# Query, key and gate products token-major as seven products of eight, retention chunk by chunk inside the last weight set, HGRN alone in stage two

## The chip, the cores and the metric

The kernel runs on one core of a Trainium2 chip. Its engines are TensorE (PE in the profile, with its weight loads as PEld), VectorE (DVE), ScalarE (ACT), GpSimd (POOL) and SyncE (SP), which here only starts transfers. Each engine runs its own queue of instructions in order. The metric is the device time of one execution in microseconds (us); of several executions the median is given. All times in this document are microseconds unless marked ns.

## What is computed

One layer of a hybrid decoder, for a prompt of 2048 tokens and for 8 single decode tokens, with a model width of 1024, all in float32:

```python
p = rmsnorm(x, norm_g) @ w_in                    # (2048, 1024) @ (1024, 4096)
rq, rk, rv, rg, hq, hf, hi, hgate = split(p, 8)  # 512 columns each: 4 heads x 128
# retention: rotary positions on q and k, a fixed decay per head
rq, rk = rotary(rq), rotary(rk) * 128 ** -0.5
o_ret = recurrence(rq, rk, rv, log_gamma)        # S = gamma*S + k v^T,  o = S^T q
o_ret = head_rmsnorm(o_ret, ret_g) * silu(rg)
# HGRN2: decay per channel, from the forget gate
f = lb + (1 - lb) * sigmoid(hf)
k = (1 - lb) * sigmoid(-hf)
o_hg = recurrence(silu(hq), k, hi, log(f))       # S = diag(f)*S + k v^T
o_hg = head_rmsnorm(o_hg, hg_g) * silu(hgate)
y = rmsnorm(x + concat(o_ret, o_hg) @ w_out, final_norm_g)
```

The states after the last token are outputs too. The decode tokens start from given states and go through the same formulas, one step each.

## The kernel before

**Products.** Every float32 operand of a large product is split into a rounded high part, written by ScalarE (`hi_lo`, L106), and the rest, written by VectorE (L107). A product of two such operands is three TensorE matmuls, high by high, high by low and low by high (`three`, L303, L305). Below, "plain" is a product done that way. "Seven products" is one step of a Strassen scheme: a product of 2x2 blocks is made from seven block products of sums of blocks instead of eight. The list is

```python
PRODUCTS = [("A11", "B11"), ("A12", "B21"), ("S2", "T2"), ("S3", "T3"), ("S1", "T1"), ("S4", "B22"), ("A22", "T4")]
```

where A is a pair of 128-token chunks (S1 to S4 its sums, made by `tok_ops` and split by `s_split`) and B the weights (T1 to T4 their sums, made by `wv_comb`). One block product is 4 x 3 = 12 matmuls of 128x512.

**The order of work.** TensorE's queue is in the order of the program's text; the queues of the other engines are ordered by a scheduler that works from the program's data. Work wrapped in `behind` (L115) is placed after the latest instruction of VectorE, ScalarE and SyncE at that point of the text.

**Stage one** computes the two value groups, rv and hi, token-major (tokens on the partitions): eight pairs of 256 tokens, in the order `V_ORDER`. Two pairs are plain, with 96 matmuls each, and six go through `v_pair` (L307) with 84. The seven results pass through seven rotating PSUM banks, VectorE adds them up, and the values are stored in `v_dram`. Norm factors (`stats`, `spread`) and splits for the next pairs are placed between the products.

**Stage two** has 16 units: for each half of the prompt (1024 tokens) and each of four head numbers, one HGRN head and then one retention head.

```python
for half in range(2):
    for h in range(NH):
        order += [(half, 1, h), (half, 0, h)]
```

A unit first computes three groups of its head feature-major (features on the partitions), plain, in segments of 512, 256 and 264 tokens in the first half, where the 264 hold the eight decode tokens, and 512 and 512 in the second (`seg_steps`, L578). The tiles are `pjqr`, `pjkr` and `pjg` for retention, `pjfh`, `pjqh` and `pjg` for HGRN. VectorE and ScalarE evacuate them: rotary tables for retention (`ret_proj`, L630), sigmoids for HGRN and gates (L612, L652 to L665). Then comes its scan. For retention: scores per chunk (L757). For HGRN: seven levels of updates, each multiplying key and query by products of forget gates (L811), kept copies by ScalarE (L821, L822), and small score products put through masks (L841, L847). Both end in `tail_steps`: key transposes (L683), key-value products (L690), the chain of states on VectorE (L698), outputs (L705, L707), squares on ScalarE (L711), the norm factor on GpSimd (L102, L103), one scaling of 128x512 (L715), output transposes (L721), a product with the gate (L723) and a store to `o_dram` (L726).

The scan of unit i is woven into the matmuls of unit i+1. `merge` walks the matmuls and puts in a scan step when its share of the work is due:

```python
while n < len(rec) and (need + rec[n][0]) * span * total <= at * due:
    need += rec[n][0]
    rec[n][1]()
    n += 1
```

Side work has places in units (`side_at`): sums of the output weights (`t_sum`, `t_spool`) and the eight decode states, with a load (`d_load`), two VectorE products, a sum and a TensorE product (`d_mm`, tile `pd`, L403). Splits of the next tokens (`x_steps`) and of the output weights (`wo_steps`) are woven into certain units.

**Stage three** is the output projection over `o_dram` and the weights: two plain chunks and seven pairs as seven products (tile `po`), the residual, the last norm, and a product for the decode tokens (`pyd`, L403), in which four strips of the 128 rows hold four column blocks.

Of the kernel before, what the change touches and what calls it, by code (L numbers as in the profile page):

```python
# [10 lines left out]
F32 = mybir.dt.float32  # L11
# [30 lines left out]
def step_kernel(ctx, tc, a, out):  # L42
# [8 lines left out]
    ps_pj = ctx.enter_context(tc.tile_pool(name="ps_pj", bufs=3, space=PSUM))  # L51
    ps_lv = ctx.enter_context(tc.tile_pool(name="ps_lv", bufs=2, space=PSUM))
    ps_o = ctx.enter_context(tc.tile_pool(name="ps_o", bufs=2, space=PSUM))
    ps_tr = ctx.enter_context(tc.tile_pool(name="ps_tr", bufs=1, space=PSUM))
# [5 lines left out]
    v_dram = [  # L60
        [dr.tile([CH, P, GW], F32, tag=f"v_dram{n}{ty}", name=f"v_dram{n}{ty}") for ty in range(2)]
        for n in range(2)
# [34 lines left out]
    rst = const.tile([P, T - 512], F32, name="rst")  # L97
    const.tile([P, 56], F32, name="fill")
    dq, dk, df, dg_ = (const.tile([P, 8, NB], F32, name=f"d{n}") for n in "qkfg")
# [28 lines left out]
    order = []  # L128
    for half in range(2):
        for h in range(NH):  # L130
            order += [(half, 1, h), (half, 0, h)]
    want = []
    for half, ty, h in order:
        for g in ((RQ, RK, RG), (HF, HQ, HG))[ty]:
            want.append(g * NH + h)
# [18 lines left out]
    x_cur = {}  # L154

    def x_alloc(blk):
        n = 528 if blk == 1 else 512
        x_cur[blk] = tuple(
            xp.tile([P, KT, n], F32R, tag=f"x{t}{blk % 2}", name=f"x{t}{blk}") for t in "hl"
        )  # L160

    def x_load(blk, kp):
        r = rawp.tile([P, 2, 512], F32, tag="raw", name=f"xr{blk}{kp}")
        for j in range(2):
            sp.dma_start(
                r[:, :, j * 256 : j * 256 + 256], a["x_t"][2 * blk + j, :, 2 * kp : 2 * kp + 2]
            )
        return r

    def x_split(blk, kp, r):  # L170
        xh, xl = x_cur[blk]
        rb = rst[:, (blk - 1) * 512 : blk * 512]
        for j in range(2):
            k = 2 * kp + j
            dve.scalar_tensor_tensor(
                r[:, j], r[:, j], g_in[:, k : k + 1], rb, op0=ALU.mult, op1=ALU.mult
            )
# [5 lines left out]
    V_ORDER = [4, 5, 6, 7, 2, 3, 0, 1]  # L183
    vctx = ExitStack()
    vq = vctx.enter_context(tc.tile_pool(name="vq", bufs=1))
    x_alloc(0)
    xh0, xl0 = x_cur[0]
# [18 lines left out]
    def bank(shape, name):  # L206
        pl, tag = ((ps_pj, "pj"), (ps_lv, "lv"), (ps_o, "o"))[(0, 1, 2, 0, 1, 2, 0)[bank_n[0] % 7]]
        bank_n[0] += 1
        return pl.tile(shape, F32, tag=tag, name=name)
# [3 lines left out]
    def tok_load(i):  # L213
        p = V_ORDER[i]
        xr[i] = [rawp.tile([P, 4, 2 * P], F32, tag="raw", name=f"xr{p}{j}") for j in range(2)]
        for j, r in enumerate(xr[i]):
            sp.dma_start(r, a["x_t"][p, :, 4 * j : 4 * j + 4])
# [1299 lines left out]
```

## Time and profile before

| | |
|---|---|
| median of 3 runs | 1065.55 (1065.42 to 1066.16) |
| span of the profiled execution | 1062.5 |
| TensorE busy in it | 1050.9 (99%), 9107 matmuls |
| VectorE busy | 733.6 (69%) |
| ScalarE busy | 395.3 (37%) |
| GpSimd busy | 115.8 (11%) |
| moved by DMA | 149.64 MB, of that 110.14 MB in SyncE's queue |
| busy at 0 to 174.3, stage one (TensorE / VectorE) | 172.7 / 139.8 |
| 174.3 to 881.0, stage two | 705.9 / 462.2 |
| 881.0 to 1062.5, last scan and stage three | 172.3 / 131.6 |

The span runs from the first to the last instruction that the profile shows. The median of the runs is 3.05 above it. The page gives the busy time of each engine, the same in 40 slices of the span (a digit is tenths), and a chain of work that ended last, followed back from the last instruction to whatever released it. A matmul's row names the tile that it fills, the tiles that it reads and its shape. Rows of groups end in the number of instructions, their busy time, the mean ns of one, and the idle time of the engine ahead of them with what ended it. Matmul records overlap, since they are pipelined, so the distance between two starts tells what one costs.

### The profile page before, as it was taken

The numbers are of one execution on the slowest core, as the hardware profiler recorded it, in microseconds if no ns is written. First come the engines' busy times: TensorE is split into PE (matmuls) and PEld (weight loads), VectorE is DVE, ScalarE is ACT, GpSimd is POOL, SyncE is SP. The second block draws the span as 40 slices with busy tenths as digits, with TensorE's granted clock in tenths as the row PEclk, the third lists the DMA queues.
The fourth block names the chain that finished last, engine by engine and source line by source line (L and its number), as shares of the span: only waits on it lengthen the run. The fifth ranks groups of instructions, "written<-read, shape, count | busy, mean of one in ns | idle before, by whom it ended". The sixth has DMA issues, their size and how long they took to land.

```text
span 1062.5 us, 21859 instructions
## 1 busy us (share of the span) xinstructions
PE 1050.9 (99%) x9107; PEld 899.6 (85%) x9107; DVE 733.6 (69%) x1271; ACT 395.3 (37%) x859; POOL 115.8 (11%) x218
## 2 busy tenths in 40 slices
PE   9999999999999999999999999999999999999997
PEld 7788888989989999998988888888788888788775
DVE  6886986594585567457977565746855687678785
ACT  7853323242432243333443323332423244333241
POOL 1110000001000010110110101011010103311122
PEclk9999999999999999999999999999999999999999
DMA  8664346422502240361654235126323337855642
GB/s 303 208 216 156 127 139 225 166 78 100 187 34 80 87 153 2 119 202 39 200 157 122 63 108 151 40 67 182 120 67 109 108 106 268 276 187 200 220 160 99
DMA packets 103890, 149.64 MB, mean 141 GB/s; under 512 B 5872, under 2 KB 69552, under 8 KB 103024
## 3 DMA queue, kind: packets, MB, share of 16 engines
q1 hardware_dynamic: 83888, 110.14, 32.9%
q0 software_dynamic: 6960, 25.24, 6.5%
q10 hardware_dynamic: 12944, 12.88, 3.5%
q8 instruction: 71, 1.16, 0.4%
q14 instruction: 27, 0.22, 0.1%
HBM read 109.86 MB, written 38.37 MB: 140 GB/s over the span
## 4 chain that ended last, share of the span: by engine, by line
PE 91%; DMA 3%; DVE 2%; ACT 2%; issue 1%; POOL 1%; SPq 0%; DVEq 0%; POOLq 0%; ACTq 0%
PE pjg L578 17%; PE po L305 13%; PE pv L305 11%; PE pjkr L578 9%; PE pjqr L578 8%; PE pjqh L578 8%; PE pjfh L578 8%; PE plh L841 2%; DMA xn<-in_x_prompt 2%; PE py L1231 1%; PE pur L690 1%; PE par L757 1%; PE por L705 1%; PE por L707 1%; PE poh L705 1%; PE puh L690 1%
## 5 line engine op out<-in xcount | busy, mean ns | idle before, releaser
L578 PE MATMUL pjg<-xh,w_h 128*128 128x512 f32 (+2 forms) x320 | 113.9, 356 | 0.0
L578 PE MATMUL pjg<-xh,w_l 128*128 128x512 f32 (+2 forms) x320 | 111.3, 348 | 0.0
L578 PE MATMUL pjg<-xl,w_h 128*128 128x512 f32 (+2 forms) x320 | 111.0, 347 | 0.0
L106 ACT ACTIVATE w_h<-wr 128x1024 fp32r<-128x1024 f32 x48 | 50.8, 1059 | 87.5 <-PE pjg L578 33.6
L107 DVE TENSOR_TENSOR w_l<-wr,w_h 128x1024 fp32r<-128x1024 f32 x48 | 58.6, 1222 | 23.3 <-ACT w_h L106 11.4
L578 PEld LDWEIGHTS pjg<-xh,w_l 128*128 128x128 f32 x320 | 60.2, 188 | 7.9
L578 PEld LDWEIGHTS pjg<-xh,w_h 128*128 128x128 f32 x320 | 60.3, 188 | 7.1 <-issue 0.4
L578 PEld LDWEIGHTS pjg<-xl,w_h 128*128 128x128 f32 x320 | 60.3, 188 | 6.7
L578 PE MATMUL pjqr<-xh,w_h 128*128 128x512 f32 (+2 forms) x160 | 58.2, 364 | 0.0
L578 PE MATMUL pjkr<-xh,w_h 128*128 128x512 f32 (+2 forms) x160 | 57.9, 362 | 0.0
L578 PE MATMUL pjfh<-xh,w_h 128*128 128x512 f32 (+2 forms) x160 | 57.4, 359 | 0.0
L821 ACT ACTIVATE kepth<-kh 128x1024 f32<-128x1024 f32 x24 | 25.5, 1062 | 85.6 <-DVE kh L811 85.6
L578 PE MATMUL pjqh<-xh,w_h 128*128 128x512 f32 (+2 forms) x160 | 56.6, 354 | 0.0
L578 PE MATMUL pjfh<-xh,w_l 128*128 128x512 f32 (+2 forms) x160 | 55.7, 348 | 0.0
L578 PE MATMUL pjkr<-xl,w_h 128*128 128x512 f32 (+2 forms) x160 | 55.5, 347 | 0.2 <-issue 0.2
L578 PE MATMUL pjkr<-xh,w_l 128*128 128x512 f32 (+2 forms) x160 | 55.6, 347 | 0.0
L578 PE MATMUL pjqh<-xh,w_l 128*128 128x512 f32 (+2 forms) x160 | 55.6, 347 | 0.0
L578 PE MATMUL pjqr<-xh,w_l 128*128 128x512 f32 (+2 forms) x160 | 55.6, 347 | 0.0
L578 PE MATMUL pjqr<-xl,w_h 128*128 128x512 f32 (+2 forms) x160 | 55.5, 347 | 0.0
L578 PE MATMUL pjqh<-xl,w_h 128*128 128x512 f32 (+2 forms) x160 | 55.5, 347 | 0.0
L578 PE MATMUL pjfh<-xl,w_h 128*128 128x512 f32 (+2 forms) x160 | 55.5, 347 | 0.0
L612 ACT ACTIVATE sg<-pjg 128x512 f32<-128x512 f32 (+2 forms) x40 | 20.4, 510 | 75.9 <-PE pjg L578 65.9
(851 smaller groups left out, 2819.5 us busy)
## 6 DMA issues: line engine op xcount, KB each, us to landing
wr<-in_w_in SPq DMA_DIRECT2D x48, 512.0 KB, 4.8
xn<-in_x_prompt SPq DMA_DIRECT2D x32, 256.0 KB, 3.0
v_dram<-vo SPq DMA_DIRECT2D x32, 256.0 KB, 2.8
v<-v_dram SPq DMA_DIRECT2D x16, 512.0 KB, 4.8
or<-o_dram SPq DMA_DIRECT2D x16, 512.0 KB, 5.8
xro<-in_x_prompt SPq DMA_DIRECT2D x14, 512.0 KB, 3.3
out_y_prompt<-xro POOLq DMA_DIRECT2D x13, 512.0 KB, 3.0
xr<-in_x_t SPq DMA_DIRECT2D x12, 512.0 KB, 4.4
```

The lines of the kernel that those rows point to most:

```text
L106: act.activation(h, src, AF.Copy)
L107: dve.tensor_tensor(l, src, h.bitcast(F32), op=ALU.subtract)
L305: pe.matmul(ps, xx, ww, start=(first and n == 0), stop=(last and n == 2))
L578: pe.matmul(ps, ww[:, kk], x[:, k, b0 : b0 + n], start=(k == 0 and i == 0), stop=(k == KT - 1 and i == 2),)
L612: act.activation(sg[:, :n], ps, AF.Sigmoid)
L690: pe.matmul(pu[:, j], ksb[g][:, j], vcol(4 * g + j), start=True, stop=True)
L705: pe.matmul(po[:, j], A[:, c], vcol(c), start=True, stop=src is None)
L707: pe.matmul(po[:, j], qcol(c), src, start=False, stop=True)
L757: pe.matmul(pa[:, j], k[:, cc], q[:, cc], start=True, stop=True)
L821: act.activation(ss[:, 512:], k[:, :HALF], AF.Copy)
L841: pe.matmul(dst[32 * i : 32 * i + 32, c], kk, qq, start=True, stop=True)
L1231: pe.matmul(ps, o[:, kk], w[:, k % 4, i * 512 : (i + 1) * 512], start=(k == 0 and n == 0), stop=(k == KT - 1 and n == 2),)
```

## The change

Stage one gets three weight sets. Set zero is the value groups as before. Set one is rq and rg, set two rk and hgate. Each set runs over all eight token pairs, so there are 24 pairs, of which the first two are plain and 22 are seven products. Stage two is left with the two HGRN groups hf and hq of each head.

- **Products.** They accumulate in three PSUM banks, a, b and c, where a product continues its bank's sum. ScalarE copies three stages out (`s1`, `u2`, `p5`). The results that go to memory are made by `emit`: gates get their SiLU there (ScalarE sigmoid, VectorE product), queries and keys their rotation (`turn`, four VectorE operations).
- **Operands of later sets.** The scaled tokens and their sums are stored by set zero and loaded again by the later sets (`a_dram`, `s_dram`); so are the weight sums of sets one and two (`wg_load`, `wg_spool` in pairs three to six of the set before; `wg_fetch` in pair seven). Their splits (`wg_split`) stand across the boundary of two sets. Set two walks the pairs in order 0 to 7, and set one in the order 1, 2, 4, 5, 3, 6, 7, 0.
- **Decode tokens.** Their query, key and gates come from 16 products in four strips (`wg_decode`) beside the weight loads.
- **Retention.** In set two, each chunk's four heads are worked through when the pair that follows computes: load of query, value and gate; transposes of key and query (`r_flip`); scores and masks; key-value products; outputs, squares, norm factor on GpSimd and scaling with the gate; transposes back, scaling by ScalarE, store. The state of four heads stays in one tile. The last chunk's steps are merged with the first steps of HGRN unit 0.
- **HGRN.** Eight units, (half, head), in stage two; the scan's steps and weights are as before. The output's scaling takes the token-major gate in four operations of 128x128 in place of one of 128x512, and the norm weight moves to ScalarE's copy of the transposed output. `side_at` halves its positions; token splits are woven into units 0, 3 and 4, output-weight splits into unit 7. The sums T2 and T1 of the output weights load into other buffers, T1 after the last scan. The products' PSUM pool has two buffers (`ps_pj`, three before), as has that of the transposes.

The diff, cut to its core:

```diff
+    CHAIN = [("A11", "B11", "a"), ("A12", "B21", "b"), ("S2", "T2", "a"), ("S1", "T1", "c"),
+             ("S3", "T3", "a"), ("S4", "B22", "c"), ("A22", "T4", "a")]
...
+    def turn(dst, src, cs, name):
...
+        dve.tensor_tensor(
+            t1[:np_].rearrange("p (h d) -> p h d", d=64), src.rearrange("p (h d) -> p h d", d=64), c, op=ALU.mult
+        )
+        dve.tensor_tensor(u[:np_, :, 1], x[:, :, 0], sn, op=ALU.mult)
+        dve.scalar_tensor_tensor(u[:np_, :, 0], x[:, :, 1], -1.0, sn, op0=ALU.mult, op1=ALU.mult)
+        dve.tensor_tensor(dst, t1[:np_], t2[:np_], op=ALU.add)
...
+        for n, (x, w, b) in enumerate(CHAIN):
...
             if n == 0:
+                keep("s1", ps)
             elif n == 1:
+                emit(ca, 0, ps, "s1")
             elif n == 2:
+                keep("u2", ps)
             elif n == 3:
+                keep("p5", ps)
             elif n == 4:
+                emit(ca + 1, 1, ps, "p5")
             elif n == 5:
+                emit(ca, 1, ps, "u2")
             else:
+                emit(ca + 1, 0, ps, None)
...
+        if p:
+            st[0] += [lambda: r_flip(cb)]
+            st[0.5] = [lambda: r_update(cb)]
+            st[1] += [lambda: r_score(cb)]
+            st[2] += [lambda: r_out(cb)]
+            st[4] += [lambda: r_turn(cb)]
+        if more:
+            st[0] += [lambda: r_load(ca, "q")]
+            st[2] += [lambda: r_load(ca, "v"), lambda: r_flip(ca)]
+            st[3] += [lambda: r_load(ca, "g"), lambda: r_score(ca), lambda: r_update(ca)]
+            st[4] += [lambda: r_load(ca + 1, "q"), lambda: r_out(ca)]
+            st[5] += [lambda: r_load(ca + 1, "v")]
+            st[6] += [lambda: r_turn(ca), lambda: r_load(ca + 1, "g")]
...
-            dve.tensor_tensor(ob[g], po, rs.unsqueeze(2).to_broadcast([P, 4, P]), op=ALU.mult)
+            for j in range(4):
+                dve.scalar_tensor_tensor(
+                    ob[g][:, j], po[:, j], rs[:, j : j + 1], gcol(4 * g + j), op0=ALU.mult, op1=ALU.mult
+                )
...
-            dve.tensor_tensor(
-                ot, pt.rearrange("p a b -> p (a b)"), gt[:, g * 512 : (g + 1) * 512], op=ALU.mult
-            )
+            act.activation(ot, pt.rearrange("p a b -> p (a b)"), AF.Copy, scale=ng[:, hd : hd + 1])
...
-    for hd, at in enumerate((8.45, 10.02, 10.48, 12.02, 12.33, 12.63, 14.02, 14.45)):
+    for hd, at in enumerate((4.22, 5.01, 5.24, 6.01, 6.16, 6.31, 7.01, 7.22)):
...
-    for k, at in enumerate((0.5, 2.1, 4.1, 6.1)):
+    for k, at in enumerate((0.5, 1.1, 2.1, 3.1)):
```

In `r_steps`, p is the pair's number in set two, ca the even chunk of this pair and cb the odd chunk of the pair before; `st[n]` holds what follows product n of the pair, and `st[0.5]` what stands in the middle of product one.

749 lines of the change are left out of this document (454 added, 295 removed).

## The prediction

> **What bounds the kernel now.** I read the page first (busy shares, slices, chain), then the chain in order of time, then the groups by shape, then stretches.
>
> ```profile
> PE 1050.9 (99%) x9107; PEld 899.6 (85%) x9107; DVE 733.6 (69%) x1271; ACT 395.3 (37%) x859; POOL 115.8 (11%) x218
> PE   9999999999999999999999999999999999999997
> DVE  6886986594585567457977565746855687678785
> PE 91%; DMA 3%; DVE 2%; ACT 2%; issue 1%; POOL 1%; SPq 0%; DVEq 0%; POOLq 0%; ACTq 0%
> ```
>
> TensorE is busy in every slice and is 91% of the chain; VectorE has a third of the span free. So a matmul taken away is worth its full distance to the next one, as long as VectorE and ScalarE still hand over in time. Distances come from the chain in order of time (start, length, what, count) and, for small ones, from the difference of two starts in the timeline:
>
> ```profile
> 61.85 19.09 PE pv L305 x84
> 174.26 5.44 PE pjfh L578 x24
> 190.58 2.84 PE pjfh L578 x24
> 199.10 2.92 PE pjfh L578 x24
> 297.61 1.40 PE pjqr L578 x6
> 344.37 2.77 PE pjfh L578 x12
> ...
> 682.19 0.60 PE L683 MATMUL pkh<-ident,kh 128*128 128x128 f32 x4
> 682.55 0.48 PE L578 MATMUL pjkr<-xh,w_h 128*128 128x512 f32 x1
> 685.40 1.05 PE L690 MATMUL puh<-v,ksh 128*128 128x128 f32 x8
> 686.29 0.60 PE L683 MATMUL pkh<-ident,kh 128*128 128x128 f32 x4
> 996.45 1.05 PE L403 MATMUL pyd<-wd,dq 128*8 128x256 f32 x16
> 997.42 0.50 PE L305 MATMUL po<-woh,op5A11h 128*128 128x512 f32 x1
> ```
>
> A 512-column matmul costs 19.09/84 = 0.227 us, one of 256 columns 2.84/24 = 0.118, of 264 columns 2.92/24 = 0.122. Four transposes take 682.55 - 682.19 = 0.36, four fp32 128x128 products (eight records) 0.89, two decode products of four strips 0.97, so 0.485 each.
>
> **What the change takes from TensorE.** Counted in the two programs' instruction orders: 512-column matmuls go from 3108 to 3300 (+192 x 0.227 = +43.6), those of 256 and 264 columns from 576 each to 192 each (-384 x 0.118 = -45.4, -384 x 0.122 = -46.7). Together -48.5: seven products of eight, for four of the six groups that were plain. It adds 64 transposes (the query's flip; the key's flip replaces the key's old transpose): 64 x 0.09 = +5.8. The decode columns of those groups become 16 four-strip products: 16 x 0.485 = +7.8. The fp32 retention and HGRN products keep their number. Net -34.9. If nothing else moved, the span would be 1062.5 - 34.9 = 1027.6. The median of the runs, 1065.55, is 3.05 above the profiled span, and I carry that offset: 1030.7 is the floor.
>
> **What becomes late.** Most of the change is on VectorE and ScalarE, which run their queues in the order written. The durations (mean ns of one, ahead of the last bar):
>
> ```profile
> L107 DVE TENSOR_TENSOR w_l<-wr,w_h 128x1024 fp32r<-128x1024 f32 x48 | 58.6, 1222 | 23.3 <-ACT w_h L106 11.4 <-DMA t_draml<-wos11l 4.5 <-DMA t_draml<-wos21l 4.3
> L811 DVE TENSOR_TENSOR kh<-kh,fph 128x512 f32<-128x512 f32 x48 | 33.3, 694 | 2.4 <-PE plh L841 1.7 <-PE plh L891 0.3
> L698 DVE SCALAR_TENSOR_TENSOR sth<-sth,fph,puh 128x128 f32<-128x128 f32 x48 | 16.7, 347 | 9.7 <-PE puh L690 8.3
> L715 DVE TENSOR_TENSOR obh<-poh,orsh 128x512 f32<-128x512 f32 x16 | 11.1, 691 | 27.7 <-ACT jkh L711 16.9 <-POOL orsh L103 10.8
> L665 DVE TENSOR_TENSOR qth<-qh,fh 128x256 f32<-128x256 f32 x8 | 3.4, 424 | 0.2
> L654 DVE TENSOR_SCALAR fh<-fsh,lb,lb 128x512 f32<-128x512 f32 x12 | 6.5, 546 | 19.2 <-ACT fsh L652 19.2
> L657 DVE TENSOR_SCALAR kh<-fxh,lb 128x512 f32<-128x512 f32 x12 | 5.8, 486 | 0.0
> L847 DVE COPY_PREDICATED Abh<-lmask,plh 128x128 f32<-128x128 uint8 x32 | 10.7, 334 | 0.3
> L821 ACT ACTIVATE kepth<-kh 128x1024 f32<-128x1024 f32 x24 | 25.5, 1062 | 85.6 <-DVE kh L811 85.6
> L822 ACT ACTIVATE kepth<-qth 128x512 f32<-128x512 f32 x24 | 15.0, 626 | 0.0
> L612 ACT ACTIVATE sg<-pjg 128x512 f32<-128x512 f32 x24 | 14.3, 594 | 55.4 <-PE pjg L578 45.4 <-DVE dS L981 5.1 <-PE pd L403 4.8
> L711 ACT ACTIVATE jkh<-poh 128x128 f32<-128x128 f32 x64 | 17.8, 278 | 10.8 <-PE poh L707 9.3
> L711 ACT ACTIVATION_READ_ACCUMULATOR jkh<-poh 128x1 f32 x64 | 12.5, 196 | 0.0
> L103 POOL TENSOR_TENSOR orsh<-orsh,mhalf 128x4 f32<-128x4 f32 x16 | 17.6, 1097 | 1.2
> L102 POOL TENSOR_SCALAR orsh<-omsh 128x4 f32<-128x4 f32 x16 | 4.1, 257 | 281.7 <-ACT jkh L711 281.6
> ```
>
> *Retention inside the third set.* A pair of chunks gives TensorE 19.09 + 24 transposes (2.2) + 32 fp32 products (7.1) = 28.4. VectorE has about 20.6 of work, so its throughput suffices, but the work is one chain through the queues from one pair's key rotation to the next. Step by step: flips 0.72, six matmuls 1.36, a wait of 0.6 (ScalarE's two copies and four key scalings take 2.3 after the first flip), key-value products 0.89, six matmuls 1.36: 4.9. Then VectorE adds 0.69, rotates (0.69 + 0.42 + 0.42 + 0.69) and masks the score with four small operations (1.4): 4.3, and only then can the output products start: 1.79, four squares with their accumulator reads 1.9, GpSimd 1.35, four scalings 1.4: 6.4. Splits (0.69 + 1.22 + 1.22) stand in the queue ahead of the second chunk's four mask operations (1.4): 4.5. Its output again: 6.4. Split 1.22, add 0.69, sigmoid 0.59, product 0.69, rotation 2.2: 5.4. Sum 31.9, against 28.4: 3.5 late per pair, for seven pairs 25, and 3 for the first, where weight splits of 1.22 stand ahead of the key. **+28** (bounds: 0 if the queue overlaps these steps, 37 if nothing does).
>
> *HGRN alone.* The scan on TensorE is what a unit of three groups took beyond them: 344.37 - 297.61 - 3 x (5.44 + 2.84 + 2.92) = 13.2. A unit of two groups is then 22.4 + 13.2 = 35.6 in half 0, 4 x 5.44 + 13.2 = 35.0 in half 1. Before, a scan had a retention unit and its own successor beside it; now each 35 us hold one. VectorE per unit: 14 updates x 0.69 = 9.7, products of forget gates 2.2 (0.69, 0.42 and smaller), masks 2.2, eight states and eight outputs x 0.347 = 5.6, gates and queries 2 x (0.546 + 0.486 + 0.69 + 0.69) = 4.8, two weight splits 2.4: 26.9. The outputs are the one row that the change makes worse there: four of 0.347 replace one of 0.691, +0.7 each. [...]
>
> Side work now falls into half as many units: output-weight sums (4 x 0.69 + 2 x 1.22 = 5.2) in units 0 to 3, token splits (4.9) in 3 and 4, decode states (2 or 3 x 1.22 each) in 4 to 7, output-weight and first output splits (7.3) in 7. VectorE then needs 32, 32, 37, 34, 32, 37, 41 in units 1 to 7 and some 36 beside the last scan. Its queue also waits inside each unit: for the first scores 1.4, for ScalarE's two keeps after each pair of updates (1.06 + 0.63, three times, partly covered), for the two output norms. Walking unit 2 and unit 6 through the written order gives waits of about 5, and unit 4 gives 11, because its decode product stands behind an update, three splits and the decode state's own steps on VectorE. Units 1 to 7 then last 37, 37, 41, 45, 37, 41, 46 and the last scan 40 (its floor 35): late by 1.5, 1.5, 5.5, 10, 2, 6, 11 and 5. **+42** (bounds: 13, the surplus of VectorE's work alone, to 55).
>
> *First two sets and joints.* The product chain now accumulates in one bank, so the seventh product waits for VectorE's read of the fifth; with spooled weight sums ahead of it (two of 0.69 and a split) that is 1.1 late in four pairs: 4.4. Two pairs of set one redo the token sums: 3. Splits between sets one and two: 2. The first HGRN unit's second token block reuses the retention's memory, so its four splits (4.9) start after the last retention output: 4. The output weights' sum T1 loads only when the last scan releases its buffers: 2. **+15** (0 to 25).
>
> Sum: 1030.7 + 28 + 42 + 15 = 1115.7; forecast 1115.
>
> **The rivals.**
> *Waits stay hidden (faster).* TensorE remains the bound, as it is in the row of 99%; only VectorE's surplus of 13 in stage two and some 3 at the joints show: 1030.7 + 16 = 1047. It decides where all new waits together stay under 33. For it speaks that VectorE kept up in this stretch at 82%, with TensorE never idle:
>
> ```profile
> 58.00:174.00 116.00, 115.81 (x523) 95.58 (x522) 95.52 (x156) 44.93 (x73) 5.01 (x12) 1.00 0.50 166
> 565.00:655.00 90.00, 90.00 (x885) 75.52 (x888) 54.15 (x95) 28.89 (x69) 9.31 (x14) 1.00 0.33 100
> ```
>
> (columns: stretch, length, busy us of PE, PEld, DVE, ACT, POOL, granted clock, DMA share, GB/s.) Against it: there the splits served a pair ahead, while stage two's 54 of 90 become 32 to 41 of 35. Chance 0.14.
> *Half the waits:* the walks count each wait in full and some overlap: 1030.7 + 85/2 = 1073, still slower. Chance 0.2.
> *Transfers bind in the first set.* Pairs three to six move tokens, norm rows, values, spooled tokens, spooled sums, new weights and their sums: seven MiB, 7.34 MB, in 20 us, 367 GB/s. The first row above gives 166/0.50 = 332 GB/s when all engines work, so 22.1 us a pair, +8, and as much where the next set's seven MiB are fetched in one pair: 1115 + 16 = 1131. Chance 0.12.
> *Waits cost clock too.* The granted clock is 1.00 in both rows, with no idle TensorE to test it. [...] Chance 0.06.
>
> **How the numbers follow.** The forecast case has 0.48. The range of 8 in 10 leaves out most of the fastest case below and the upper bounds together above (1030.7 + 37 + 55 + 25 = 1148): 1053 to 1148. A measurement of this kernel tells about 0.2% from no change (1063.4 to 1067.7). Faster 0.14 from the first rival; same 0.04 from the low edge of half the waits; slower 0.82.
>
> **What would show it.** Right: TensorE's share falls from 99% to near 92%, with idle time ahead of the retention's output and flip products released by VectorE, and ahead of the HGRN kept-score, decode and output transposes; pairs of the third set last about 32, HGRN units 37 to 46; VectorE above 85% in stage two. Wrong: pairs of 28.5 and units of 36, or long DMA waits in the first set. The forecast falls if the whole new idle time of TensorE is under 50 us.

## The result, and the profile after

The changed kernel takes 1136.03 us (median of 4 runs, 1131.52 to 1138.34) against 1065.51 before, a ratio of 1.0653 with a 95% interval of 1.0628 to 1.0678. The profiled execution took 1131.52, 1.8 above its span of 1129.7. The forecast was 1115 with a range of 1053 to 1148: the direction and the range held, and the time is 21 above the forecast.

The page of the changed kernel: busy shares, then four of the rows of 40 slices, the transfers, and the chain that ended last, as shares of the span.

```profile
PE 1059.6 (94%) x8731; PEld 866.8 (77%) x8731; DVE 795.5 (70%) x1453; ACT 525.9 (47%) x1153; POOL 149.7 (13%) x260
PE   9999999899998999999996799997998998899997
DVE  6867756887768665566555587786668688567776
PEclk9999999999999999999998899998999998999999
DMA  8698889477778555555444934476445573865652
DMA packets 141625, 235.73 MB, mean 209 GB/s; under 512 B 10224, under 2 KB 78080, under 8 KB 141264
PE 27%; issue 6%; DVE 4%; ACT 3%; DMA 3%; POOL 2%; POOLq 0%; ACTq 0%; DVEq 0%; SPq 0%
```

TensorE is no longer full in every slice: the deepest holes are the 22nd and 23rd (unit 0, at 594 to 640), the 28th, and smaller ones between the 31st and the 35th. The granted clock falls in four of these slices; in the two stretches that the prediction showed of before it was 1.00. VectorE's share is what it was (69%, now 70%). The bytes moved grew from 149.64 to 235.73 MB, and in the first third of the span the transfers are mostly at seven to nine tenths. (The chain can be followed back only to 612 us, so its shares are of half a span.) TensorE stands idle for 1129.7 - 1059.6 = 70.1 us, where it was 1062.5 - 1050.9 = 11.6 before. Line numbers from here on are lines of the changed kernel or of the edit in question.

The stretches of the changed kernel, in the order sets zero and one, set two, unit 0, units 1 to 7, last scan, projection (columns as in the prediction: stretch, length, busy us of PE, PEld, DVE, ACT, POOL, granted clock, DMA share, GB/s):

```profile
0.00:350.70 350.70, 342.16 (x1631) 269.71 (x1632) 253.21 (x421) 164.25 (x296) 29.87 (x52) 1.00 0.79 281
350.70:594.10 243.40, 233.22 (x1324) 198.33 (x1323) 151.75 (x326) 123.68 (x347) 30.12 (x45) 0.99 0.54 174
594.10:640.10 46.00, 34.44 (x319) 30.62 (x317) 27.80 (x57) 18.53 (x42) 5.62 (x8) 0.85 0.63 204
640.10:931.60 291.50, 267.49 (x4218) 222.82 (x4209) 219.71 (x445) 147.40 (x320) 40.40 (x63) 0.96 0.54 171
931.60:980.80 49.20, 40.72 (x600) 33.12 (x598) 33.86 (x62) 24.93 (x54) 15.23 (x26) 0.92 0.54 165
980.80:1129.70 148.90, 141.58 (x655) 112.23 (x654) 109.17 (x144) 47.15 (x95) 28.44 (x67) 0.98 0.53 184
```

The boundaries are the starts of the first matmul of pair 16, of unit 0 and of unit 1, the end of unit 7's last matmul into `pjqh`, and the last HGRN output transpose. Unit lengths below are distances between such starts: 41.7, 37.5, 40.3, 52.0, 38.3, 44.6 and 37.2 for units 1 to 7.

What TensorE waited for in the changed kernel (engine, line, releaser: us in total, times, longest):

```profile
PE pkt L662 <- DVE rk L338: 11.1, 9, 5.4
PE poth L942 <- DVE obh L935: 9.7, 8, 4.9
PE pjfh L831 <- ACT fxh L873: 5.7, 1, 5.7
PE pah L1050 <- DVE qh L884: 5.5, 3, 2.3
PE pd L530 <- DVE dqp L1173: 4.8, 1, 4.8
```

These are hand-overs that the prediction named (key transposes, output transposes, first scores, decode products), and between them one product that waits for its bank's sigmoids (third row; more on it below). Behind the four longest of these, of 4.8 and more, the granted clock is 0.50 (after that of 5.7 until 627.93). The timeline of TensorE in unit 0, after its longest wait:

```profile
622.00 0.58 PE L831 MATMUL pjfh<-xh,w_h 128*128 128x256 f32 x1 [5.66 <-ACT fxh L873]
622.38 0.42 PE L831 MATMUL pjfh<-xl,w_h 128*128 128x256 f32 x1
...
627.93 0.29 PE L831 MATMUL pjqh<-xh,w_h 128*128 128x256 f32 x1
628.05 0.28 PE L831 MATMUL pjqh<-xl,w_h 128*128 128x256 f32 x1
```

Matmuls of 256 columns are 0.21 apart until 627.9 and 0.12 after it. This happens at ten places. The granted clock of those stretches is 0.50. TensorE is busy for 40.6 us in them, and half of that, 20 us, is what half speed costs it.

### The profile page after: what moved, and what is told of

Read it like the earlier page. It is cut to its first block, busy times and chain, and to the rows that moved or that the text cites. A ratio compares the mean times of both kernels' runs of the same rounds, so it can differ in the third digit from the quotient of the medians.

```text
span 1129.7 us, 22331 instructions
## 1 busy us (share of the span) xinstructions
PE 1059.6 (94%) x8731; PEld 866.8 (77%) x8731; DVE 795.5 (70%) x1453; ACT 525.9 (47%) x1153; POOL 149.7 (13%) x260
## 2 busy tenths in 40 slices
DMA packets 141625, 235.73 MB, mean 209 GB/s; under 512 B 10224, under 2 KB 78080, under 8 KB 141264
## 5 line engine op out<-in xcount | busy, mean ns | idle before, releaser
L1001 DVE TENSOR_TENSOR kh<-kh,fph 128x512 f32<-128x512 f32 x48 | 33.3, 693 | 13.2 <-PE plh L1031 12.4
L699 DVE SCALAR_TENSOR_TENSOR obr<-por,omr,rg 128x128 f32<-128x128 f32 x64 | 18.0, 344 | 34.6 <-POOL omr L697 34.6
L113 DVE TENSOR_TENSOR ab_l<-xr,ab_h 128x512 fp32r<-128x512 f32 (+1 forms) x40 | 38.1, 955 | 5.1 <-ACT ab_h L112 3.9
L831 PEld LDWEIGHTS pjfh<-xh,w_h 128*128 128x128 f32 x160 | 31.8, 199 | 11.3 <-ACT fxh L873 5.8
L112 ACT ACTIVATE ab_h<-xr 128x512 fp32r<-128x512 f32 (+1 forms) x40 | 32.5, 848 | 15.9 <-DVE xr L270 15.8
L831 PEld LDWEIGHTS pjqh<-xh,w_h 128*128 128x128 f32 x160 | 31.0, 194 | 8.6 <-ACT w_h L112 2.9
L831 PEld LDWEIGHTS pjfh<-xh,w_l 128*128 128x128 f32 x160 | 31.8, 199 | 4.5
L831 PEld LDWEIGHTS pjfh<-xl,w_h 128*128 128x128 f32 x160 | 32.0, 200 | 3.4
L113 DVE TENSOR_TENSOR w_l<-wr,w_h 128x1024 fp32r<-128x1024 f32 x16 | 19.5, 1221 | 20.9 <-ACT w_h L112 14.8
L831 PEld LDWEIGHTS pjqh<-xl,w_h 128*128 128x128 f32 x160 | 31.1, 194 | 3.0
L1523 DVE SCALAR_TENSOR_TENSOR xro<-xro,yms,fg 128x1024 f32<-128x1024 f32 (+1 forms) x15 | 18.1, 1214 | 21.2 <-POOL yms L109 21.2
L1004 DVE TENSOR_TENSOR qth<-qth,fph 128x512 f32<-128x512 f32 x48 | 32.8, 684 | 0.0
```

Of the source, the lines that this page charges most:

```text
L112: act.activation(h, src, AF.Copy)
L113: dve.tensor_tensor(l, src, h.bitcast(F32), op=ALU.subtract)
L699: dve.scalar_tensor_tensor(o[:, cc], po[:, h], ms[:, h : h + 1], rb_of[c, "g"][:, cc], op0=ALU.mult, op1=ALU.mult)
L831: pe.matmul(ps, ww[:, kk], x[:, k, b0 : b0 + n], start=(k == 0 and i == 0), stop=(k == KT - 1 and i == 2),)
L1001: dve.tensor_tensor(kv[:, :, 0, :], kv[:, :, 0, :], two[:, :, 1:2].to_broadcast([P, nb, b]), op=ALU.mult)
L1004: dve.tensor_tensor(qv[:, :, 1, :], qv[:, :, 1, :], two[:, :, 0:1].to_broadcast([P, nb, b]), op=ALU.mult)
```

## The experiments

All twelve are edits of the changed kernel, to be compared with its 1136.0; three (own buffers, scores, all together) stand each on the edit before it and are compared with that run. The times are medians, with the fastest and slowest run behind them. Lengths of stretches and units come from one profiled execution each. That of the changed kernel is the fastest of its four, and sets zero and one, which nearly all the edits leave alone, took 350.7 to 353.9 us in the profiles (but for one run, named below), so a difference of 3 us in one stretch tells nothing. The kernel before, run again beside the edits, took 1065.6 to 1067.2 us.

### Half speed: idle matmuls ahead of seven waits

```diff
+    def keep_warm(n):
+        t = ps_tr.tile([P, P], F32, tag="tr", name=f"kw{warmed[0]}")
+        for _ in range(n):
+            pe.matmul(t, ident, ident, start=True, stop=True)
...
+            if p == 0:
+                st[2] += [lambda: keep_warm(20)]
```

> The changed kernel with idle matmuls added: small fp32 products of the identity into a spare transpose buffer, placed just ahead of seven of its longest TensorE waits (20 before the first key transposes of the retention, 8 before those of its last chunk, 24 after its last output transposes, 12 before the first kept scores of unit 1, 20 before the decode product of unit 4, 8 and 20 before the second output transposes in unit 3 and in the last scan). Nothing is computed differently and no wait is removed. Theory: a wait costs twice, once for itself and once because the granted clock is 0.50 in the stretch of 3.4 us or more behind it. In the profile after, such stretches behind these seven places cost TensorE 2.0 + 1.7 + 3.0 + 1.6 + 2.7 + 1.7 + 1.4 = 14 us; they go: 1136 - 14 = 1122. Rival: what follows a wait is late through VectorE anyway, so a faster TensorE only waits longer: 1136, within 3 us.

Measured: 1135.5 (1133.0 to 1136.0). The granted clock of the changed kernel, and of this run:

```profile
core 0: 1129.7 us, clock 0.976
```

```profile
core 0: 1133.7 us, clock 0.991
```

The clock came back and the time did not. The rival holds for the sum: TensorE now waits 9.9 us at one place, the kept scores of unit 4, where the changed kernel waits 0.3 (and 4.8 and 2.5 at other places of that unit), and unit 4 is 55.7 instead of 52.0. A faster TensorE only arrives earlier at something else that is late.

### Three hand-overs moved

```diff
-            st[2] += [lambda: r_load(ca, "v"), lambda: r_flip(ca)]
+        if more and p == 0:
+            st[3] += [lambda: r_load(ca, "g"), lambda: r_flip(ca)]
...
-                if n in (1, 2, 3, 5, 7):
+                for _ in range({3: 1, 4: 2, 5: 1, 7: 1}.get(n, 0)):
...
-    wd_at[2] += [(0, d_ms), (2, d_rs), (4, d_tr)]
+    wd_at[2] += [(0, lambda: behind(d_ms)), (2, d_rs), (4, d_tr)]
```

> The changed kernel with three hand-overs moved, no work removed. One: in the first pair of set two the transposes of the first chunk, its scores and its outputs each stand one product later, its transposes back half a pair later. Two: the last chunk's steps, merged with the first matmuls of unit 0, start two matmul steps later and then follow each other closely. Three: in the last scan the decode norm's square on ScalarE stands behind what was issued before it, and GpSimd starts the loads of T1 only after the last scan's stores. Theory: each is a single late hand-over that the order of the queues makes, with the halved clock behind it: 5.4 + 2.0 at the first place, 2.5 + 1.7 and some 4 at the second, some 5 + 1.4 at the third: 22 in all: 1136 - 22 = 1114. Rival: VectorE is behind there as a whole, and the waits come back at the next hand-over: 7 less or nothing: 1129 to 1136.

Measured: 1136.2 (1133.9 to 1138.0). The first pair of set two got shorter (30.7 to 28.0) and so did unit 0 (46.0 to 44.7) and the last scan (49.2 to 47.1), but sets zero and one took 3.0 more in the profiled execution and the projection 4.6 more. The three places are 6 shorter together and the two other stretches 7.6 longer, of which the 3.0 lie where nothing was edited, so by the median the rival's "nothing" holds, and the profile can't say more.

### VectorE: less work

One edit gives an operation to ScalarE, the other halves the updates of the scans.

```diff
-            dve.tensor_scalar(k[:, tt], xr[:, :n], lb1[:, h : h + 1], None, op0=ALU.mult)
+            act.activation(k[:, tt], xr[:, :n], AF.Copy, scale=lb1[:, h : h + 1])
```

> The changed kernel with one VectorE operation of each HGRN evacuation given to ScalarE: the key's scaling by one minus the lower bound, 20 operations of 0.35 to 0.49 us, 8.6 us of VectorE in all. Theory (order of hand-overs, VectorE busy at 74% of stage two): what stands behind these operations comes earlier only where VectorE is the last: some 3 us less, 1133. Rival (VectorE's throughput bounds the units): the whole 8.6 us, 1127.

Measured: 1139.3 (1133.9 to 1141.5), no gain.

```diff
+            nh = nb // 2
-                kv[:, :, 0, :], kv[:, :, 0, :], two[:, :, 1:2].to_broadcast([P, nb, b]), op=ALU.mult
+                kv[:, :nh, 0, :], kv[:, :nh, 0, :], two[:, :nh, 1:2].to_broadcast([P, nh, b]), op=ALU.mult
```

> The changed kernel with each of the 112 update operations of the HGRN scans on half of its blocks (the other half of the keys and queries is left as it is), 0.3 us less for each; every instruction, transfer and dependency stays. Theory: VectorE's chain of updates sets the pace of a unit: 14 x 0.3 = 4.3 less per scan, as far as the units' TensorE work allows (6.1, 1.9, 4.3, 4.3, 3.3, 4.3, 2.2 and 4.3): 31 less, 1105. Rival: weights, tokens and other transfers set it, and VectorE only waits longer: 8 less, 1128.

Measured: 1135.6 (1134.4 to 1136.9). One of the two groups of updates in the changed kernel, and in this run, by shape:

```profile
L1001 DVE TENSOR_TENSOR kh<-kh,fph 128x512 f32<-128x512 f32 x48 | 33.3, 693 | 13.2 <-PE plh L1031 12.4 <-PE plh L1081 0.5
```

```profile
L1002 DVE TENSOR_TENSOR kh<-kh,fph 128x256 f32<-128x256 f32 x48 | 20.3, 424 | 21.2 <-PE plh L1032 18.4 <-ACT kepth L1012 2.6
```

The updates fell from 693 to 424 ns, and the idle time ahead of them rose from 13.2 to 21.2. Units 1 to 7 of this run:

```profile
645.40:936.70 291.30, 266.49 (x4218) 222.86 (x4209) 197.81 (x445) 146.85 (x321) 40.97 (x63) 0.97 0.54 170
```

VectorE is busy 198 us instead of 220, and the stretch is 291.3 where the changed kernel has 291.5. Only single units moved, some up and some down (units 1, 4 and 6 by -2.6, -2.7 and -2.7, unit 5 by +5.0). VectorE's amount of work does not set the pace of stage two.

### Side work and stores

```diff
-        steps = [d_load, lambda hd: d_mul(hd, 0), lambda hd: d_mul(hd, 1), d_add, d_mm]
+        side_at.append((at, lambda hd=hd: d_load(hd)))
+        side_at.append((at + 0.25, lambda hd=hd: d_skip(hd)))
...
-    for k, at in enumerate((0.5, 1.1, 2.1, 3.1)):
```

> The changed kernel without the side work of stage two: the sums and splits of the output weights and the products of the decode states are left out (their loads of states and their stores of states stay; other stored sums are loaded in their place, so the later stages keep their transfers). Token splits stay. Theory (my walk): the side work that now falls into half as many units is what makes units late: units 1 to 7 go from 41.7, 37.5, 40.3, 52.0, 38.3, 44.6, 37.2 to about 37, 36.5, 38, 41, 37, 37, 36.5, so 28 less, and unit 0 some 2 less: 1136 - 30 = 1106. Rival: a scan of HGRN alone under two groups of matmuls is late by its own chain of updates, and the side work only fills its gaps: the units stay at 40 or more, 8 less in all: 1128.

Measured: 1124.4 (1122.0 to 1126.3). The total, 11.6 less, is nearer the rival's 1128 than the theory's 1106. Units 1, 4, 6 and 7 are 37.6, 41.7, 39.4 and 34.5, 22 less together, as the theory said. But unit 5 went from 38.3 to 47.2, and its timeline shows where 4.9 of that went:

```profile
813.25 0.68 PE L1031 MATMUL plh<-qth,kh 128*32 128x16 f32 x61
818.85 0.19 PE L1031 MATMUL plh<-qth,kh 128*32 128x16 f32 x1 [4.92 <-issue]
```

Ahead of the last of 64 small products TensorE stands still for 4.9 us and waits for nothing that the profile names. Around it, from 804 to 820, the transfers fill nine tenths or more of 34 of 40 slices, states being loaded and stored without the products that used to space them, and among the queues is one that the page calls instruction:

```profile
DMA  9989999999999977999999999999999999788999
q1 hardware_dynamic: 7486, 4.66, 96.3%
q8 instruction: 2, 0.03, 0.7%
```

Whether the last instruction itself came late by that queue, no run shows.

```diff
-        for x, y in zip("hl", split((t, ra)[n].rearrange("p a b -> p (a b)"), f"wos{k}{n}")):
-            pool.dma_start(t_dram[x, n][:, :, k], y.bitcast(F32).rearrange("p (a b) -> p a b", a=2))
+        split((t, ra)[n].rearrange("p a b -> p (a b)"), f"wos{k}{n}")
```

> The changed kernel without the stores of the output-weight sums, 8 MiB in units 0 to 3 (their sums and splits are still made; other stored sums are loaded in their place). No work of an engine but the stores' issue is taken away. Theory: transfers hold up stage two, by full queues (99% busy at 751 to 767 in the profile after) and by weight buffers that wait for these stores: units 0, 1, 3 and 4 lose 2 each: 8 less, 1128. Rival: VectorE's and ScalarE's own work does: within 3 of 1136.

Measured: 1124.7 (1122.1 to 1127.5): 11.3 less, though every sum and split is still made. (The transfers at 751 to 767, called 99% busy there, had a DMA share of 0.97.) Units 1 and 4 go from 41.7 and 52.0 to 36.4 and 46.6. How a store holds up a scan can be read in unit 1. The changed kernel's stores of the first sum's two halves, issued at 634.78 and 636.13 (the last figure is us from issue to landing), and the chain that ended last behind them (start, length, what):

```profile
t_dramh<-wos00h POOLq DMA_DIRECT2D x1, 512.0 KB, 7.0
t_draml<-wos00l POOLq DMA_DIRECT2D x1, 512.0 KB, 8.2
```

```profile
641.86 1.07 ACT w_h L112
...
644.37 1.22 DVE w_l L113
645.59 0.61 DVE kh L1001
```

The split sum shares its buffers with the weights. The high half lands at 634.78 + 7.0 = 641.8, and the next weight's high part starts at 641.86; the low half lands at 636.13 + 8.2 = 644.3, and the weight's low part starts at 644.37. The scan's updates stand behind the low part in VectorE's queue, which was idle for 4.47 us ahead of it, and the first of them starts at 645.59, when it ends. ScalarE's timeline without the stores:

```profile
640.01 0.37 ACT L883 ACTIVATE qsh<-pjqh 128x264 f32<-128x264 f32 x1
640.28 1.05 ACT L112 ACTIVATE w_h<-wr 128x1024 fp32r<-128x1024 f32 x1
```

No wait, and the weight is split at once. So VectorE is late here because its queue holds, ahead of the updates, an instruction that waits for a transfer, not because of what it computes.

### SyncE's order, buffers, scores, and all moves together

```diff
-            r = rawp.tile([P, D], F32, tag="raw", name=f"wr{n}")
-            sp.dma_start(r, a["w_in"][j])
-            w_ready.append(split(r, f"w{n}_"))
+            w_raw(n + 1)
+            w_ready.append(split(w_raws[n], f"w{n}_"))
+            if n > 1:
+                w_raw(n + 2)
...
+            behind(get)
...
-        sp.dma_start(out[("new_ret_sample", "new_hgrn_sample")[ty]][0, :, h].rearrange("b d v -> d b v"), S)
+        act.dma_start(out[("new_ret_sample", "new_hgrn_sample")[ty]][0, :, h].rearrange("b d v -> d b v"), S)
```

> The changed kernel with SyncE's queue in stage two put in another order, the same transfers: raw weights are loaded one group earlier, the loads of values and gates of a scan stand behind what was issued before them, and the stores of decode states go to ScalarE's queue behind the copy that follows their product. Theory: in the profile after, SyncE's queue, which runs in order, stands still at such transfers (15.7 us at the values of unit 0, 12 at a store of unit 5, 11 at a store of unit 6), the weight loads behind them are issued late, and the weight splits then hold up the queues of ScalarE (22 us) and VectorE (19 us) ahead of the scan's updates. Units 1, 4 and 6 go from 41.7, 52.0, 44.6 to about 39, 44, 39: 17 less in all: 1119. Rival: the scan's own chain through VectorE and ScalarE ends last, weights or not: 4 less, 1132.

Measured: 1147.8 (1143.6 to 1151.0), 12 more; both sides missed. Units 2, 5 and 6 and the last scan got longer (39.1, 42.0, 47.4, 52.7). Units 1 and 4, which were to gain most, took 41.7 and 52.7. Which of the three parts cost most was not tried.

```diff
+        hl = [pools["ex"].tile([P, D], F32R, tag="wos" + x, name=f"wos{k}{n}{x}") for x in "hl"]
+        hi_lo(*hl, (t, ra)[n].rearrange("p a b -> p (a b)"))
```

> The run before (SyncE's order) and besides that buffers of their own for the splits of the output-weight sums, which share the three weight buffers in the changed kernel, so that a weight split waits for the store of such a sum to land. Theory: the weight split at 641.9 in the profile after waits 4.2 us for that; unit 1 loses 3 more and the rest 2: 5 less than the run before. Rival: none of it shows, within 2 us of the run before.

Measured: 1141.5, 6.3 less than the run before, as the theory said; unit 1 went from 41.7 to 38.9 and unit 4 from 52.7 to 49.4. It is the wait that the run without stores took away, though not the whole of it: the buffers are one of each kind, and in unit 0 the split of the second sum now waits for the first one's store (1.9 us on VectorE at 644.3).

```diff
-        steps = [(0, scores0), (2.3, lambda: scores(1)), (0, load), (2.3, lambda: scores(3)), (2.3, scores3)]
+        steps = [(0.6, scores0), (2.3, lambda: scores(1)), (0, load), (2.3, lambda: scores(3)), (2.3, scores3)]
```

> The run before (SyncE's order, own buffers) and besides that the first scores of each HGRN scan placed one matmul step (6 matmuls, 1.36 us) into the next unit rather than at its start. The query is now the last group of a unit (before the change the gate was), so its last segment is evacuated while TensorE already stands at these scores: 1.2 to 2.5 us in each of eight scans in the profile after. Theory: this wait is on the path: 1.5 x 8 = 12 less than the run before. Rival: the same evacuation holds the updates that follow, and the wait comes back at the kept scores: 3 less or none.

Measured: 1140.5, 1.0 less than the run before. The rival holds. Unit 0 is 7.7 shorter and unit 1 is 5.7 longer, but most of that is the boundary: the first scores, 5.8 us with their wait, now stand in unit 1. Units 4 and 6 are 2.7 shorter and 3.4 longer.

The last of them adds the three moved hand-overs shown above to these three edits, with no edit of its own.

> The run before (SyncE's order, own buffers, scores later) and besides that the three moved hand-overs of the earlier run, which gave nothing by themselves (first transposes of the retention later, last chunk's steps closer, last scan's norm factors and T1 loads). Theory: they gave nothing where a late weight came after them and took up what they saved; with the weights early they give 8 less than the run before. Rival: the waits at these places are bound by other things (memory that the last retention output still holds, VectorE's splits): 2 less or none.

Measured: 1137.3 (1137.0 to 1140.9), 3.3 less than the run before, between the two, with overlapping runs. All four edits together end where the changed kernel stands, 1136.0.

### Stage two cut to its HGRN units

```diff
-        (3, 1): lambda: x2[:3],
-        (3, 2): lambda: x2[3:],
-        (4, 0): lambda: x_steps(3),
+        (3, 2): lambda: [lambda: x_cur.update({2: x_cur[0], 3: x_cur[1]})],
...
+            sp.dma_start(
+                out[f"new_{st}_sample"][0, :, h].rearrange("b d v -> b d v"), a[f"state_{st}"][0, :, h]
+            )
```

> The changed kernel with stage two cut to its HGRN units: the sums of the output weights, the decode states (their given states are copied out instead) and the token blocks of the second half (the first half's splits are used again) are left out; other stored sums are loaded for the output projection, so that it keeps its transfers. Theory: an HGRN scan alone under two groups of matmuls nearly fits, and what makes units late is what stands beside it, splits and transfers. Units 1 to 7 and the last scan, 340.8 in the profile after, go to 37 each and 45: 304, unit 0 loses 2: 38 less, 1098. Rival: the scan's own chain through VectorE and ScalarE is longer than a unit's matmuls: units stay at 39 and more, 15 less, 1121.

Measured: 1155.4 (1152.3 to 1157.6), 19 more, with less to do. Two things happened. In stage two, units 1 to 7 and the last scan take 317.2 instead of 340.8, between the two theories: units of 37.6, 38.1, 40.9, 39.9, 38.4, 40.3 and 34.6, and 47.4. About 24 us of the lateness belonged to the side work and its transfers; units without any still take some 23 more (269.8 for units 1 to 7) than their TensorE work by the prediction's prices, 246.8. TensorE stands idle for 13.4 of these 23, of which 8.5 are waits for the query at first scores and 3.7 waits for scaled outputs ahead of transposes; half speed is 4.2, and the rest is TensorE work above its price. And the eight copies of states from memory to memory, 512 KB each, were issued not in stage two but from 30.6 to 267 us, where the scheduler put them. The first stretch, and its longest waits of TensorE:

```profile
0.00:391.40 391.40, 354.90 (x1630) 275.68 (x1631) 254.16 (x421) 166.55 (x296) 22.35 (x52) 0.96 0.75 262
```

```profile
PE prs L257 <- DVE dg L252: 15.7, 5, 9.9
PE pgd L530 <- DMA wgr<-in_w: 8.6, 3, 7.2
```

With the eight copies, sets zero and one are 40.7 longer (391.4 against 350.7), 5 us for each: norm factors and weights that feed TensorE came late. Whether it is their place in SyncE's queue, whose order changed with them, or the bytes that cost it, the run does not tell; the transfers' share of this stretch is 0.75, less than the 0.79 of the changed kernel.

### Without the retention

```diff
-            st[0] += [lambda: r_flip(cb)]
-            st[0.5] = [lambda: r_update(cb)]
-            st[1] += [lambda: r_score(cb)]
-            st[2] += [lambda: r_out(cb)]
+            st[2] += [lambda: r_put(cb)]
```

> The changed kernel without the retention (its transposes, scores, states, outputs and their loads are left out; the rotated keys are stored in place of its outputs). What it takes with it is the whole price of the retention inside set two. Theory: 24 transposes and 32 products were priced at 2.2 + 7.1 = 9.3 us of TensorE per pair beside 19.09 for the products, so pairs of 30.3 hold some 1 us of waits each, and the rest of the lateness is at the two ends: pairs go to 19.8, which set one has where nothing stands beside it, set two from 243.5 to 8 x 19.8 = 158, and unit 0 from 46.0 to its own 22.4 and some waits for splits, 26: 105 less, 1031. Rival: the lateness at the ends belongs to the weight splits of the joint and to the token splits of unit 0, retention or not: set two 166, unit 0 at 34: 89 less, 1047.

Measured: 1040.2 (1038.1 to 1042.5), 95.9 less, between the two. Two pairs' first matmuls in the timeline, in this run and then in the changed kernel:

```profile
397.79 0.39 PE L316 MATMUL pv18a<-wv_h,ab_h 128*128 128x512 f32 x1
...
417.07 0.39 PE L316 MATMUL pv19a<-wv_h,ab_h 128*128 128x512 f32 x1
```

```profile
411.96 0.48 PE L316 MATMUL pv18a<-wv_h,ab_h 128*128 128x512 f32 x1
...
442.29 0.48 PE L316 MATMUL pv19a<-wv_h,ab_h 128*128 128x512 f32 x1
```

In the changed kernel TensorE waits in six pairs, from the one before this on (381 to 564 us), only for these two, 0.6 a pair:

```profile
PE pkt L662 <- DVE rk L338: 2.2, 6, 0.6
PE por L683 <- DVE rA L672: 1.4, 6, 0.2
```

A pair is 417.07 - 397.79 = 19.28 without the retention and 442.29 - 411.96 = 30.33 with it, so that the retention's own TensorE work is 30.33 - 19.28 - 0.6 = 10.4. Of the 95.9 won, set two gave 81.5 (243.4 to 161.9) and unit 0 gave 16.5 (46.0 to 29.5); the other stretches stayed within 2, but for unit 1, which lost 3.5. The first pair of set two is 26.9 even without the retention, 7.6 more than those behind it: the rival is right there, this lateness belongs to the joint of sets one and two with its weight splits. Unit 0, at 29.5, is nearer the theory's 26 than the rival's 34: its chunk was priced at 4.7, and 16.5 went with it.

## Why the prediction was right and where it missed

By stretches, each priced as the prediction did, with the floor first (sets zero and one: 174.3 + 8 x 19.09 + 7.8; set two: 8 x 28.4 less the last output's 4.7, which falls into unit 0; last scan and projection: what is left of 1027.6):

| stretch | floor | measured | late | predicted late |
|---|---|---|---|---|
| sets zero and one | 334.8 | 350.7 | 15.9 | 9.4 |
| set two | 222.5 | 243.4 | 20.9 | 28 |
| unit 0 | 27.1 | 46.0 | 18.9 | 4 |
| units 1 to 7 | 246.8 | 291.5 | 44.7 | 37 |
| last scan and projection | 196.4 | 198.1 | 1.7 | 7 |
| sum | 1027.6 | 1129.7 | 102.1 | 85.4 |

**The sign held, and new waits made it.** They outweigh the work that was taken away: TensorE's idle time grew by 70.1 - 11.6 = 58.5, above the 50 below which the forecast was to fall, and key transposes, output transposes and decode products were among the places named. TensorE's share was to fall to near 92% and fell to 94%; the slower clock counts as busy, which hides 20 us.

**Mis-sized: the floor.** TensorE was to lose 34.9 of its 1050.9. Its busy time is 1059.6, and without the 20.3 of half speed 1039.3: only 11.6 came off. So the 102.1 are 58.5 of new waits, 20.3 of half speed and 23.3 of TensorE work above its price. About 8 of these are the retention's in set two (next paragraph), 9 stand in sets zero and one and 11 in units 1 to 7, against some 9 less in the table's last row, whose floor is only what is left over. A pair of seven products in set two without the retention came out near its price, 19.28 for 19.09; why the work elsewhere costs more was not tried.

**Mis-sized: the retention's pairs.** Predicted 31.9, measured 30.3. TensorE's work beside the products was 10.4, not 9.3, and the waits 0.6, not 3.5: the walk through the queues added steps that overlap. The joint ahead of the pairs was given 3 and cost the 7.6 of the run without retention. The two together, 7 x (30.3 - 28.4) + 7.6 = 21, are the row of set two.

**Mis-sized: unit 0.** It was given the four splits, 4. What is late is the memory. GpSimd, ScalarE and SyncE in the changed kernel's timeline, around the last retention output, and what SyncE's queue waited for ahead of that load (us in total, times, longest):

```profile
617.92 0.81 POOL L711 DMA_DIRECT2D o_dram<-obr  x1 [3.13 <-ACT obr L710]
```

```profile
620.86 0.60 ACT L872 ACTIVATE fsh<-pjfh 128x512 f32<-128x512 f32 x1 [2.25 <-issue]
```

```profile
620.90 0.38 SPq L854 DMA_DIRECT2D v<-v_dram  x1
```

```profile
SPq L854 <- DMA o_dram<-obr: 15.7, 1, 15.7
```

The store of the last retention output took 2.8 us from issue to landing, so it landed at 617.92 + 2.8 = 620.7. The first sigmoid and the first load of values start at once behind that, at 620.86 and 620.90, the load released by that store, and TensorE's product waits 5.66 for the sigmoid. By these times the first scan's tiles lie in memory of the retention's buffers that is free only when the store has landed. The prediction released the memory with the output, not with its store. No run took the store alone away; that unit 0 is 16.5 shorter without the retention is shown.

**The step that failed: what makes stage two late.** The size was near (45 for 37) by luck. The 37 were all to be waits; in the trace the 44.7 are 23.9 of idle TensorE, 9.3 of half speed and 11.5 of work above its price. And the waits have another cause than the one given. The prediction built them from VectorE's surplus of work and put VectorE above 85%. VectorE is busy 219.7 of 291.5 there, 75%. Taking 22 us from it moved nothing, and neither did moving work to ScalarE. What did move the units was transfers: the stores of the weight sums (-11.3 by leaving them out, -6.3 against the run before by giving them buffers of their own) and the side work with its loads and stores (23.6 of units 1 to 7 and the last scan; how much of that is the transfers and how much the work is not divided). Where a weight's split waits for a transfer in the queues of ScalarE and VectorE, the scan stands behind it: in unit 1 for the stores shown above, and in unit 4 for the load of the weight itself:

```profile
768.82 1.06 ACT L112 ACTIVATE w_h<-wr 128x1024 fp32r<-128x1024 f32 x1 [5.71 <-DMA wr<-in_w_in]
```

```profile
769.91 1.23 DVE L113 TENSOR_TENSOR w_l<-wr,w_h 128x1024 fp32r<-128x1024 f32 x1 [5.32 <-ACT w_h L112]
```

The next update on VectorE starts at 771.05, behind that split. The prediction's walk did count waits "through the written order", but not these. The price that the walk put on an output scaling of 128 columns, 0.347, stood as the row has it:

```profile
L935 DVE SCALAR_TENSOR_TENSOR obh<-poh,orsh,v 128x128 f32<-128x128 f32 x64 | 18.0, 343 | 21.6 <-POOL orsh L109 19.3 <-ACT qsh L883 2.3
```

An output scaling of 128 columns took 343 ns.

**The rivals.** *Waits stay hidden* and *half the waits* are wrong by the time: 102 were late, not 16 or 43. (The waits alone, 58.5, lie between the second rival's 43 and the forecast's 85.) *Transfers bind in the first set* is not shown. Sets zero and one are 16 late at a DMA share of 0.79, where the rival had 16 on top of 9 of other lateness. But of TensorE's 8.5 us of idle time there, the waits that name a transfer are 0.6 and those that name VectorE 6.8; whether transfers stand behind VectorE's lateness was not followed. That eight added copies made these sets 40.7 later shows only that they have little to spare. *Waits cost clock too* happened, at ten places. TensorE in the timeline, at the last key transposes, in unit 0:

```profile
596.77 0.40 PE L831 MATMUL pjfh<-xh,w_l 128*128 128x512 f32 x1
599.62 0.66 PE L662 MATMUL pkt<-ident,rk 128*128 128x128 f32 x4 [2.45 <-DVE rk L338]
...
600.47 0.64 PE L831 MATMUL pjfh<-xh,w_h 128*128 128x512 f32 x1
600.90 0.63 PE L831 MATMUL pjfh<-xl,w_h 128*128 128x512 f32 x1
```

A wait of 2.45 was enough: the 512-column products behind it are 0.43 apart instead of 0.23. The ten half-speed stretches are 3.41 long, or twice or three times that. In this trace's clock records the ten stretches start at whole multiples of 3.413 us from one another. In the window of that length just ahead of each, TensorE was idle for 1.5 to 3.4 us, and of the windows at full speed no other had more than 1.6 idle. So in this trace half speed goes with the idle time inside one window rather than with the length of a wait, though without a clean limit (1.48 was enough in the window at 931.72, 1.60 was not in that at 204.68): a wait of 1.99 (at 756.73) was followed by half speed, and one of 2.96 (at 206.28), which falls into two windows with 1.36 and 1.60, was not. The 20 us of half speed were real and worth nothing: with the clock mostly restored, the time was 1135.5.

**What stays open.** Units with no side work are still 23 above their priced TensorE work. The larger waits there are for the query and for scaled outputs, and no run took those away alone. The change also left the products two PSUM buffers of three, and no run gave the third back; the wait of 5.66 in unit 0 is one for such a buffer. The three parts of the edit of SyncE's order were not tried one by one, nor was the stall of 4.9.

## What to carry to other kernels

When an engine at 99% is given less work, ask of every instruction in the other engines' queues which transfer it may have to wait for, and when the buffers of that transfer come free: VectorE, busy for 75% of units 1 to 7, was late in them without any shortage of time. To tell the two apart, take work away from the suspected engine: if its idle time grows instead of the total falling, as here (13.2 to 21.2 ahead of the halved updates), the cause lies ahead of it. And a stretch that already runs at a high DMA share, 0.79 here, should not be given more transfers without a measurement: with eight added ones it took 391.4 us where it had taken 350.7, by their bytes or by their place in the queue.

## What had not been expected of the hardware

TensorE's clock was halved at ten places, behind windows of 3.41 us in which TensorE had been idle for as little as 1.5 us, and giving it back (mean clock 0.976 to 0.991) brought no time. TensorE stood still for 4.92 us between two of 64 like instructions, waiting for nothing that the profile names, while the packets of one queue took 96.3% of the DMA engines' time. And eight copies of 512 KB from memory to memory, whose results no engine waits for, went with 5 us each in the sets that already ran at a DMA share of 0.79.
